# A projection's first column pair goes from eight block products to seven, and all four pairs start with the products on the first half of x

## The chip, the cores and the metric

The kernel runs on one core of a Trainium2 chip. Its metric is the time of one execution on the device, in microseconds (us). The profile is that of one execution; its times are counted from the first instruction. TensorE appears as PE, its weight loads as PEld, VectorE as DVE, ScalarE as ACT, GpSimd as POOL, SyncE's DMA queue as SPq.

## The reference

One decoder layer on 1024 prompt rows and 8 sample rows of 1024 channels. Everything starts from one normalised input and one combined projection, whose columns are cut into seven parts of 1024:

```python
xn = _rmsnorm(h, pre_g)
proj = jnp.einsum('bld,de->ble', xn, w_in)
u, v, z_a, x_b, z_b, g_a, g_b = jnp.split(proj, SPLITS, axis=-1)
u = jax.nn.gelu(u)
vn = _layernorm(jax.nn.gelu(v), ln_g, ln_b)
y_a = u * _chunk_spatial_mix(vn, w_s, b_s) * jax.nn.silu(z_a)
...
m = (jax.nn.sigmoid(g_a) * jnp.einsum('ble,ed->bld', y_a, w_pa)
     + jax.nn.sigmoid(g_b) * jnp.einsum('ble,ed->bld', y_b, w_pb))
h = h + _rmsnorm(jnp.einsum('bld,de->ble', m, w_out), post_g)
e = jnp.einsum('blp,pd->bld', p, w_ple)
gate = jax.nn.sigmoid(jnp.einsum('bld,de->ble', _rmsnorm(h, ple_in_g), w_pg))
h = h + _rmsnorm(gate * e, ple_out_g)
```

The change is in the projection to v, the first of the seven to be computed.

## The kernel before

**Products.** Each part of the projection is made in four *pairs* of 256 output channels. For a pair the weights are a 2x2 grid of blocks (A11 to A22: two halves of 128 output channels by two halves of 512 input channels) and x, held transposed in the tile `big`, a 2x2 grid too (B11, B21: prompt rows 0 to 511; B12, B22: rows 512 to 1023 and the 8 sample rows, 520 columns). One block product (`product`) is 12 matmuls of 512 columns, or 24 of 260 for the wide right half, because each operand is cut (`split`) into a high and a low part and three of the four combinations are summed. ACT writes the high part, DVE the low.

**Strassen and classical.** `strassen` makes a pair in seven products, P1 to P7, in place of eight. It needs sums of weight blocks (S1 to S4, DVE, in `Weights.prepare`) and sums of x blocks (T1 to T4: `Operand.combine` on DVE, then `Operand.cut`). The T sums are made once and serve every pair of all seven parts; they can only be made once all of x has been normalised and turned. So pair 0 of v goes through `classical` instead: eight products, two at a time into one PSUM tile, first the two on the first half of x (A11·B11 + A12·B21, then the same with A21 and A22), later the two on the second half. ACT copies each of the four sums to the output tile. Pairs 1 to 3 of v, and all later parts, go through `strassen`, where P1's result is copied by ACT to a tile `u`, DVE adds P6 and P7 to it, and three more DVE adds give the outputs.

**The opening, written out by hand.** `begin` fixes the order of each engine up to about 44 us: loads, the embedding product for rows 0 to 511 (`embed`, `embed_out`), the square sums, roots and scalings of the x rows (`norm_root`: square on ACT, a DVE addition, a power on POOL; `norm_scale` on DVE), their transposes (`x_half`: PE into PSUM, ACT writes the high part, DVE the low part), and the copies that rebuild the whole of x in `big` (`x_out` on ACT from PSUM, `x_whole` on POOL from the two parts). `x_extra` turns the 8 sample rows, `p_turn` the rows of p, `x_tail` cuts the 8 sample columns. Pair 0's first two sums run between the first and the second half of x.

**PSUM.** There are three regions (`region`, two banks each) and two single banks (`bank`). A new tile takes the one whose last user comes first in the program, and waits for that user (`Planner.wanted`):

```python
over = [(max(o.seq for o in self.users[n]), n) for n in live]
old = min(x for x in over if x[0] < first.seq)[1]
first.before.update(self.users[old])
```

**After the opening** a planner (`Planner.order`) orders each engine's instructions by due times; PE's may pass each other where their data allow. `run_stream` asks for weights six steps ahead (`FETCH`) and prepares operands three steps ahead (`AHEAD`). All SBUF tiles of this phase are drawn from 46 slots of one row each. Finished pairs of v are turned to token order by copies to 16-bit planes on ACT, transposing DMAs, and copies back to `big` (`v_planes`, `v_join`, `v_turn`).

Of the kernel before, what the change touches and what calls it, by code (L numbers as in the profile page):

```python
# [15 lines left out]
P = 128  # L16
# [291 lines left out]
def hybrid_step(  # L308
# [199 lines left out]
    class Weights:  # L508
# [13 lines left out]
        def sums(self):  # L522
            if not self.kept:
                self.kept = [slot(f"{self.name}s", (P, 2, 4, P)) for _ in range(2)]
            return self.kept

        def prepare(self, what):

            w = slot(f"{self.name}w", (P, 2, 4, P), F32R)
            hi, lo = w[:, 0], w[:, 1]  # L530
            if what[0] == "A":
                split(self.quarter(int(what[1]) - 1, int(what[2]) - 1), hi, lo)
            elif what == "S2":
                s1, s4 = self.sums()
                add(s1[:, 0], self.quarter(1, 0), self.quarter(1, 1))
                sub(s1[:, 1], s1[:, 0], self.quarter(0, 0))
                sub(s4[:, 0], self.quarter(0, 1), s1[:, 1])
                split(s1[:, 1], hi, lo)
            elif what == "S3":
                s3 = self.sums()[1][:, 1]  # L540
                sub(s3, self.quarter(0, 0), self.quarter(1, 0))
                split(s3, hi, lo)
            else:
                split(self.sums()[0 if what == "S1" else 1][:, 0], hi, lo)
            self.ready[what] = hi, lo

    class Features:
# [72 lines left out]

    def classical(weights, operand, user):

        steps, regions = [], {}
        for j in range(2):
            for m in range(2):
                names = [f"A{m + 1}{k + 1}" for k in range(2)]

                def prepare(names=names):
                    for n in names:
                        if n not in weights.ready:  # L630
                            weights.prepare(n)

                def run(names=names, j=j, m=m):
                    first = m == j == 0
                    ps = regions[m, j] = bank("acc").unsqueeze(1) if first else region("acc")
                    for i, n in enumerate(names):
                        product(Features, ps, weights.ready[n], operand, f"B{i + 1}{j + 1}", i == 0, i == 1,
                                late=m == 0)

                def evacuate(j=j, m=m):  # L640
                    user.direct(m, j, Features.view(regions[m, j], j == 1))

                steps.append(Step(prepare, run, evacuate))
        steps[0].loads = lambda: (weights.fetch(), user.loads())
        steps[-1].after.append(user.finish)
        return steps

    def strassen(weights, operand, user, form=Features, order=None):
# [6 lines left out]
                ("P3", "S4", "B22", "r4"))  # L655
        place = {p: r for p, _, _, r in plan}
        halved = order is not None and order[-1] == "P2"

        def evacuate(p):
            ps = None if halved and p == "P1" else form.view(at[place[p]], p not in ("P1", "P2", "P4"))  # L660
            if p == "P1":
                both = slot("u", form.sums)
                at["u"], at["u7"] = both[:, 0], both[:, 1]
                if form.tail:
                    nc.gpsimd.memset(at["u"][:, HALF:], 0.0)
                for i, c in enumerate(CUTS if halved else ()):
                    nc.scalar.activation(out=at["u"][:, c], in_=at["r1"][i][:, :QUART], func=AF.Copy)
                if not halved:
                    nc.scalar.activation(out=at["u"][:, :HALF], in_=ps, func=AF.Copy)
                return  # L670
            u, u7 = form.like(at["u"]), form.like(at["u7"])
            if p == "P6":
                add(u, ps, u)
                at["whole"] = True
                if "r3" in at:
                    evacuate("P7")
            elif p == "P2":
                user.direct(0, 0, ps)
            elif p == "P7":
                if "whole" in at:  # L680
                    add(u7, ps, u)
            elif p == "P5":
                user.summed(1, 1, ps, u7, u7)
            elif p == "P4":
                user.summed(1, 0, ps, at["u7"][:, :HALF])
            else:
                user.summed(0, 1, ps, u)

        for p, a, b, r in sorted(plan, key=lambda x: order.index(x[0])) if order else plan:
            def run(p=p, a=a, b=b, r=r):  # L690
                new = r not in at
                if new:
                    at[r] = form.new()
                product(form, at[r], weights.ready[a], operand, b, new, True, not new)

# [10 lines left out]
            steps.append(Step(lambda a=a: weights.prepare(a), run_halves if halved and r == "r1" else run, done))  # L706
        steps[0].loads = lambda: (weights.fetch(), user.loads())
        steps[-1].after.append(user.finish)
        return steps

    class User:
# [7 lines left out]
        def loads(self):  # L719
            pass  # L720

        def outs(self):
# [134 lines left out]
    def x_half(j, kp):  # L857

        if kp == (NB // 2 - 1 if j else 0):
            ps = [bank("pst") for _ in range(2)]  # L860
        else:
            ps = region("pst")
            ps = [ps[:, kk] for kk in range(2)]
        for kk in range(2):
            k = 2 * kp + kk
            for i in range(4):
                nc.tensor.transpose(ps[kk][:, i * P : (i + 1) * P], xts[4 * j + i][:, k * P : (k + 1) * P], ident)
        hi, lo = x_parts(j, kp)
        for kk in range(2):
# [31 lines left out]
    def x_tail():  # L901
        for kp in range(NB // 2):
            split(quarter(kp, 1)[:, :, HALF:], *(x[:, :, HALF:] for x in x_parts(1, kp)))
# [42 lines left out]
    class V(User):  # L946
        turns = [[7, 0, 1], [2, 3, 4], [5, 6]]

    lnv = {}
# [328 lines left out]
    vsteps, vusers, vweights = [], [], []  # L1278
    for i, (w, u) in enumerate(pairs_of(V0, V, "v")):
        vsteps.append((strassen if i else classical)(w, xop, u))  # L1280
        vusers.append(u)
        vweights.append(w)
# [25 lines left out]
    every = lambda groups: [s for g in groups for p in g for s in p]  # L1308
    steps = [s for p in vsteps + gasteps for s in p] + every(usteps)
    late = []  # L1310
# [6 lines left out]

    c = vsteps[0]
    at(c[0], lambda: xop.combine("T3"))
    at(c[0], lambda: (xop.combine("T1"), xop.combine("T2")))  # L1320
    at(c[1], lambda: xop.cut("T2"))
    at(c[1], lambda: xop.combine("T4"))
    at(c[2], lambda: xop.cut("T3"))
    at(c[3], lambda: xop.cut("T1"))
    at(vsteps[1][0], lambda: xop.cut("T4"))

# [3 lines left out]
    for i, u in enumerate(vusers):  # L1330

        nxt = vsteps[1][1:] + vsteps[2] if i == 0 else (vsteps[i + 1] if i + 1 < NPAIR else gasteps[0])
        at(nxt[0], lambda u=u, i=i: v_turn(u.out, i, [S]))
        at(nxt[0], lambda u=u, i=i: v_planes(u.out, i))
        for m in range(2):
            at(nxt[2 + m], lambda u=u, i=i, m=m: v_join(u.out, i, m))
        for s, ts in zip(nxt[4:], V.turns):
            at(s, lambda i=i, ts=ts: v_turn(None, i, ts))
# [383 lines left out]
    def begin():  # L1722
# [9 lines left out]
        dma(xe[:NS], x_sample)  # L1732
        steps[0].loads()
        for t in range(4, NB):
            x_load(t)
# [3 lines left out]
        praw.append(psl)  # L1739
        steps[4].loads()  # L1740
        fetched[0] = 5
        early_loads()
# [5 lines left out]

        for h in range(2):
            p_new(h)  # L1750
        busy(5)
# [39 lines left out]
        for kp in range(3):  # L1791
            x_half(0, kp)
        vweights[0].prepare("A12")
        x_half(0, 3)
        steps[0].run()
        steps[1].prepare()
        norm_root(4)
        norm_root(S)
        norm_root(5)
        norm_scale(4)  # L1800
        norm_root(6)
# [5 lines left out]
        x_whole(0, 1)  # L1807
        steps[0].evacuate()
        x_out(0, 3)
        x_out(0, 2)  # L1810
        steps[1].run()
        x_extra()
        steps[1].evacuate()
        p_turn(1, 0)
        x_half(1, 0)
        p_turn(1, 1)
        x_half(1, 1)
        x_tail()
        embed(4)
        x_half(1, 2)  # L1820
        x_whole(1, 0)
        embed_out(4)
        x_half(1, 3)
        x_whole(1, 1)
        x_out(1, 2)
        x_out(1, 3)
        embed(5)
        embed_out(5)
        prepared[0] = 4
        steps[2].run()  # L1830
        steps[2].evacuate()
        embed(6)
        embed_out(6)

# [10 lines left out]
    plan.fixed = False  # L1845
    for s in range(3):
        for f in steps[s].after:
            f()
    at(steps[3], embed_rest)
    at(steps[8], embed_rows)  # L1850
    at(steps[14], embed_sample)
    run_stream(steps, 3)
    plan.play(tc)
# [30 lines left out]
```

## Time and profile before

| | |
|---|---|
| median of 3 runs | 977.66 us (977.46 to 977.98) |
| the profiled execution | 978.18 us |
| its span, first to last instruction | 976.1 us |
| PE busy in the span | 965.9 us |
| mean granted TensorE clock | 0.998 of full speed |

An engine is busy while an instruction of it runs. The span leaves out 2.08 us of the execution's own time. A row of the timeline gives the start, the duration, the engine, the operation and its tiles, and in brackets the idle time of the engine before it with what ended it; a row with "xN" merges N neighbours of one kind, and its duration runs from the first's start to the last's end.

### The profile page before, as it was taken

Reading aid. Unit: us, or ns where it says so; the run is one execution under the profiler, and the core shown is the slowest. Engines: PE = TensorE matmul, PEld = TensorE weight load, DVE = VectorE, ACT = ScalarE, POOL = GpSimd, SP = SyncE. Lnnn points to the kernel's source line nnn. Section 1 sums busy time; section 2 is a strip of 40 time slices with the busy share of each in tenths; the row PEclk is TensorE's granted clock in tenths of the full one; section 3 lists DMA queues with packets and bytes.
Section 4 is the critical chain, followed back from the end, with each engine's and each line's share of the span. In section 5 each row is a group of like instructions: output and inputs, shape, how many; then the busy total and the mean of one; then the engine's idle time right before and its main releaser. Section 6 shows DMA issues by size and latency. Waiting matters only on the chain. (4 is left out here: it accounts for less than half of the span.)

```text
span 976.1 us, 16062 instructions
## 1 busy us (share of the span) xinstructions
PE 965.9 (99%) x6089; PEld 861.1 (88%) x6089; DVE 797.1 (82%) x1256; ACT 530.7 (54%) x897; POOL 78.7 (8%) x144
## 2 busy tenths in 40 slices
PE   9999999999999999999999999999999999999996
PEld 6898999999999999999999999999999986888775
DVE  6894768777789698979797987697699899769786
ACT  6888997565434333344443343552363273977662
POOL 1500000000000000001000100000000000312222
PEclk9999999999999999999999999999999999999999
DMA  9437354322483353766735076884583392899876
GB/s 330 144 120 181 91 153 152 111 99 78 141 287 130 105 188 108 249 196 216 257 132 181 30 248 231 278 309 152 177 302 105 131 348 88 176 282 363 262 216 194
DMA packets 111914, 183.97 MB, mean 188 GB/s; under 512 B 28959, under 2 KB 68343, under 8 KB 111830
## 3 DMA queue, kind: packets, MB, share of 16 engines
q1 hardware_dynamic: 109710, 175.53, 53.0%
q0 software_dynamic: 2080, 7.41, 4.2%
q8 instruction: 48, 0.79, 0.3%
q14 instruction: 28, 0.23, 0.1%
q10 hardware_dynamic: 48, 0.01, 0.0%
HBM read 124.27 MB, written 53.87 MB: 182 GB/s over the span
## 5 line engine op out<-in xcount | busy, mean ns | idle before, releaser
L301 DVE TENSOR_TENSOR u<-acc,u 128x520 f32<-128x520 f32 (+1 forms) x90 | 62.4, 694 | 31.9 <-PE acc L301 29.3
L301 POOL TENSOR_TENSOR rstd<-ms,mhalf 128x1 f32<-128x1 f32 (+1 forms) x36 | 30.3, 843 | 225.4 <-DVE ms L301 225.1
L301 POOL MEMSET u<- 128x8 f32 x35 | 3.7, 108 | 502.9 <-PE acc L301 235.3
L301 ACT ACTIVATE u<-acc 128x512 f32<-128x512 f32 x39 | 23.3, 597 | 25.9 <-PE acc L301 25.1
L301 ACT ACTIVATE paw<-pas 128x512 fp32r<-128x512 f32 x16 | 10.1, 628 | 30.9 <-DVE pas L301 25.6
L301 ACT ACTIVATE pbw<-pbs 128x512 fp32r<-128x512 f32 x16 | 9.9, 628 | 28.6 <-DVE pbs L301 25.4
L301 DVE TENSOR_TENSOR big<-big 128x1024 f32<-128x1024 f32 (+4 forms) x20 | 23.6, 1211 | 0.0
L301 ACT ACTIVATE big<-mix 128x256 f32<-128x256 f32 x32 | 12.0, 383 | 18.6 <-PE mix L301 18.0
L301 PE MATMUL accm<-qh,wpoolw 128*128 128x260 f32 (+1 forms) x96 | 21.0, 320 | 0.0
L301 ACT ACTIVATE big<-v 128x1024 uint16<-128x1024 uint16 x16 | 18.3, 1174 | 3.0 <-DMA v<-vw 3.0
L301 ACT ACT_TABLE_LOAD x13 | 16.7, 1283 | 5.1 <-PE acc L301 2.7
L301 ACT ACTIVATE zbw<-zbs 128x512 fp32r<-128x512 f32 x16 | 10.1, 628 | 16.8 <-DVE zbs L301 10.5
L301 DVE TENSOR_TENSOR acc<-acc,u 128x512 f32<-128x512 f32 (+1 forms) x16 | 11.1, 696 | 8.8 <-PE acc L301 8.8
L301 ACT ACTIVATE gbw<-gbs 128x512 fp32r<-128x512 f32 x16 | 10.0, 626 | 14.7 <-DVE gbs L301 12.5
L301 DVE TENSOR_TENSOR big<-mix,big 128x256 f32<-128x256 f32 x32 | 12.8, 420 | 6.1 <-ACT big L301 5.6
L301 PEld LDWEIGHTS accm<-qh,wpoolw 128*128 128x128 f32 x96 | 15.6, 188 | 1.9
L301 ACT ACTIVATE zaw<-zas 128x512 fp32r<-128x512 f32 x16 | 10.1, 628 | 13.2 <-PE acc L301 5.2
L301 ACT ACTIVATE gb<-gb 128x1032 f32<-128x1032 f32 (+1 forms) x8 | 6.8, 853 | 19.1 <-DVE gb L301 19.1
L301 ACT ACTIVATE u<-u 128x1032 f32<-128x1032 f32 (+1 forms) x8 | 6.8, 853 | 18.9 <-DVE u L301 18.8
L301 ACT ACTIVATE uw<-us 128x512 fp32r<-128x512 f32 x16 | 10.0, 627 | 12.6 <-DVE us L301 8.3
L301 ACT ACTIVATE za<-za 128x1032 f32<-128x1032 f32 (+1 forms) x8 | 6.8, 855 | 17.4 <-DVE za L301 17.3
L301 ACT ACTIVATE vw<-v 128x1024 uint16<-128x1024 uint16 x16 | 16.0, 1045 | 0.0
(674 smaller groups left out, 3607.6 us busy)
## 6 DMA issues: line engine op xcount, KB each, us to landing
ga<-ga SPq DMA_DIRECT2D x16, 516.0 KB
gb<-gb SPq DMA_DIRECT2D x16, 516.0 KB
ya<-za SPq DMA_DIRECT2D x8, 516.0 KB
yb<-zb SPq DMA_DIRECT2D x8, 516.0 KB
x<-in_x_prompt_dram SPq DMA_DIRECT2D x8, 512.0 KB
vraw<-in_w_in_dram SPq DMA_DIRECT2D x8, 512.0 KB
e<-e SPq DMA_DIRECT2D x8, 512.0 KB
garaw<-in_w_in_dram SPq DMA_DIRECT2D x8, 512.0 KB
```

The costliest lines, as they stand in the source:

```text
L301: getattr(getattr(self.nc, e), method)(*args, **kwargs)
```

## The change

Pair 0 of v is made by `strassen` too, and `classical` goes. All four pairs take a new order, `AHEAD_OF` = P1, P2, P6, P7, P4, P5, P3. P1 and P2 need only B11 and B21, the first half of x: they run for pairs 0 and 1 in the opening, where pair 0's first two sums stood, and for pairs 2 and 3 right behind the opening, before any product on a T sum. P1 and P2 share a single bank; between them ACT copies P1 into the second half of the pair's own output tile (`V.sum_in`), where it waits for P6, and after P2 ACT copies the finished block to the first half. The weights come as two sides of 128 output channels (`Sides`); pairs 1 to 3 load the first side twice. B12 is no longer cut, since no product uses it: the second half of x's first four channel blocks is only copied to `big`, by ACT from PSUM, and the two `x_whole` on POOL for it go. Pair 0's weight sums and T3 are made at the end of the opening.

```diff
+        def add_up(self):
+            self.added = True
+            s1, s4 = self.sums()
+            add(s1[:, 0], self.quarter(1, 0), self.quarter(1, 1))
+            sub(s1[:, 1], s1[:, 0], self.quarter(0, 0))
+            sub(s4[:, 0], self.quarter(0, 1), s1[:, 1])
...
+    class Sides(Weights):
...
+        def side(self, m):
+            self.sides[m] = slot(f"{self.name}raw", (P, 2, 4, P))
+            for k in range(2):
+                dma(self.sides[m][:, k], self.src[k * HALF : (k + 1) * HALF, m * P : (m + 1) * P]
+                    .rearrange("(k p) m -> p k m", p=P))
+
+        def fetch(self):
+            for m in range(0 if self.again else 1, 2):
+                self.side(m)
...
+    AHEAD_OF = ("P1", "P2", "P6", "P7", "P4", "P5", "P3")
...
-                    at[r] = form.new()
-                product(form, at[r], weights.ready[a], operand, b, new, True, not new)
+                    at[r] = bank("acc").unsqueeze(1) if ahead and r == "r1" else form.new()
+                product(form, at[r], weights.ready[a], operand, b, new, True, not new, late=ahead and p == "P1")
...
-        if kp == (NB // 2 - 1 if j else 0):
+        if kp == 0:
             ps = [bank("pst") for _ in range(2)]
...
+        if j and kp < 2:
+            turned[j, kp] = ps
+            return
...
-        for kp in range(NB // 2):
+        for kp in range(2, NB // 2):
             split(quarter(kp, 1)[:, :, HALF:], *(x[:, :, HALF:] for x in x_parts(1, kp)))
...
     class V(User):
         turns = [[7, 0, 1], [2, 3, 4], [5, 6]]
+
+        def sum_in(self, i, form):
+            self.out = [*(self.out or ()), slot(self.key)]
+            return self.out[i][:, HALF:]
...
-    steps = [s for p in vsteps + gasteps for s in p] + every(usteps)
+    steps = [vsteps[i][j] for pairs in ((0, 1), (2, 3)) for j in range(2) for i in pairs]
+    steps += [s for p in vsteps for s in p[2:]] + [s for p in gasteps for s in p] + every(usteps)
...
-        vweights[0].prepare("A12")
+        vweights[1].prepare("A11")
         x_half(0, 3)
         steps[0].run()
-        steps[1].prepare()
+        vweights[0].prepare("A12")
+        vweights[1].prepare("A12")
         norm_root(4)
+        steps[0].evacuate()
+        steps[1].run()
         norm_root(S)
         norm_root(5)
+        steps[1].evacuate()
         norm_scale(4)
...
-        steps[0].evacuate()
+        steps[2].run()
+        steps[2].evacuate()
         x_out(0, 3)
         x_out(0, 2)
-        steps[1].run()
+        steps[3].run()
+        for t in (8, 4, 5):
+            steps[t].loads()
+        steps[8].loads = None
         x_extra()
-        steps[1].evacuate()
+        steps[3].evacuate()
+        p_new(1)
         p_turn(1, 0)
-        x_half(1, 0)
+        x_half(1, 2)
         p_turn(1, 1)
-        x_half(1, 1)
+        x_half(1, 3)
         x_tail()
         embed(4)
-        x_half(1, 2)
-        x_whole(1, 0)
-        embed_out(4)
-        x_half(1, 3)
-        x_whole(1, 1)
         x_out(1, 2)
+        x_half(1, 0)
+        x_out(1, 0)
+        embed_out(4, nc.vector)
         x_out(1, 3)
+        x_half(1, 1)
+        x_out(1, 1)
+        vweights[0].add_up()
+        xop.combine("T3")
         embed(5)
         embed_out(5)
         prepared[0] = 4
-        steps[2].run()
-        steps[2].evacuate()
-        embed(6)
-        embed_out(6)
```

## Rows read from the trace of the kernel before

**Rows 1.** The page's first part: each engine's busy time, share and instructions.

```profile
PE 965.9 (99%) x6089; PEld 861.1 (88%) x6089; DVE 797.1 (82%) x1256; ACT 530.7 (54%) x897; POOL 78.7 (8%) x144
```

**Rows 2.** Windows: stretch, length, busy PE, PEld, DVE, ACT, POOL; clock, DMA share, GB/s.

```profile
44.00:62.00 18.00, 18.00 (x126) 16.79 (x125) 18.00 (x23) 13.00 (x21) 0.01 (x1) 1.00 0.30 112
62.00:100.00 38.00, 38.00 (x252) 33.66 (x251) 25.67 (x36) 33.42 (x60) 1.10 (x1) 1.00 0.61 153
100.00:150.00 50.00, 50.00 (x343) 45.91 (x342) 35.38 (x62) 46.43 (x95) 1.67 (x4) 1.00 0.45 118
```

**Rows 3.** Timeline of PE: first matmuls of P5, P1, P3 and P6 in v.

```profile
75.49 0.40 PE L301 MATMUL acc<-xT1h,vw 128*128 128x260 f32 x2
...
78.37 0.39 PE L301 MATMUL acc<-xB11h,vw 128*128 128x512 f32 x1
...
81.15 0.40 PE L301 MATMUL acc<-xB22h,vw 128*128 128x260 f32 x2
...
84.03 0.40 PE L301 MATMUL acc<-xT2h,vw 128*128 128x260 f32 x2
```

**Rows 4.** Timeline of PE in and behind the opening (p_turn twice, embed twice, P6).

```profile
33.86 0.66 PE L301 MATMUL pp<-ident,p 128*128 128x128 f32 x4
...
35.58 0.60 PE L301 MATMUL pp<-ident,p 128*128 128x128 f32 x4
...
36.81 0.48 PE L301 MATMUL e<-wehi,ph 128*128 128x512 f32 x1
...
41.32 0.48 PE L301 MATMUL e<-wehi,ph 128*128 128x512 f32 x1
...
63.98 0.40 PE L301 MATMUL acc<-xT2h,vw 128*128 128x260 f32 x2
```

**Rows 5.** Timeline of ACT in the opening.

```profile
25.30 1.09 ACT L301 ACTIVATE squares<-x 128x1024 f32<-128x1024 f32 x1
...
30.50 0.57 ACT L301 ACTIVATE v<-acc 128x512 f32<-128x512 f32 x1
30.98 2.37 ACT L301 ACTIVATE big<-pst,gvec 128x512 f32<-128x512 f32 x4
33.44 0.60 ACT L301 ACTIVATE v<-acc 128x512 f32<-128x512 f32 x1
...
37.41 1.28 ACT L301 ACTIVATE xB12h<-pst,gvec 128x512 fp32r<-128x512 f32 x2
```

**Rows 6.** Timeline of DVE in the opening.

```profile
14.93 1.22 DVE L301 COPY e<-e 128x1024 f32<-128x1024 f32 x1
...
30.71 4.21 DVE L301 TENSOR_SCALAR x<-x,rstd 128x1024 f32<-128x1024 f32 x3
34.84 0.40 DVE L301 TENSOR_TENSOR big<-pxe,gvec 128x16 f32<-128x16 f32 x4
...
39.01 1.40 DVE L301 SCALAR_TENSOR_TENSOR xB12l<-pst,gvec,xB12h 128x512 fp32r<-128x512 f32 x2
```

**Rows 7.** The tile x: its scalings on DVE, ns min/median/max.

```profile
L301 DVE TENSOR_SCALAR x<-x,rstd x8: 744/752/2725, 13.9 to 32.2; 128x1024 f32<-128x1024 f32 x8
```

**Rows 8.** Timeline of POOL in the opening: two of the four x_whole.

```profile
31.84 5.32 POOL L301 TENSOR_TENSOR big<-xB11h,xB11l 128x1024 f32<-128x1024 f32 x2
```

**Rows 9.** Timeline of DVE behind the opening.

```profile
46.68 6.92 DVE L301 TENSOR_TENSOR big<-big 128x1040 f32<-128x1040 f32 x6
...
61.26 2.38 DVE L301 TENSOR_TENSOR xT3l<-big,xT3h 128x1040 fp32r<-128x1040 f32 x2
...
69.40 1.22 DVE L301 TENSOR_TENSOR xT1l<-big,xT1h 128x1040 fp32r<-128x1040 f32 x1
...
78.58 0.70 DVE L301 TENSOR_TENSOR v<-acc,u 128x520 f32<-128x520 f32 x1 [0.99 <-PE acc L301]
```

**Rows 10.** Groups of DVE, 62 to 150 us: count, busy us, mean ns, idle before.

```profile
L301 DVE TENSOR_TENSOR vw<-vs,vw 128x512 fp32r<-128x512 f32 x11 | 7.3, 679 | 0.7 <-ACT vw L301 0.7
```

More of the change, by code (lines that the diff above doesn't have):

```diff
@@ L525, in sums @@
             return self.kept
+        added = False
+        def add_up(self):
[4 more added lines that the diff above has]
+            sub(s4[:, 0], self.quarter(0, 1), s1[:, 1])
         def prepare(self, what):
@@ L533, in prepare @@
             elif what == "S2":
[L534 to L538, printed above, removed]
+                if not self.added:
+                    self.add_up()
+                split(self.kept[0][:, 1], hi, lo)
             elif what == "S3":
@@ L545, in prepare, with __init__, quarter @@
             self.ready[what] = hi, lo
+    class Sides(Weights):
+        def __init__(self, src, name, again=True):
+            super().__init__(src, name)
+            self.again, self.sides = again, {}
+        def side(self, m):
[6 more added lines that the diff above has]
+                self.side(m)
+        def quarter(self, m, k):
+            return self.sides[m][:, k]
     class Features:
@@ L619, in hybrid_step @@
     nothing = lambda: None
[L621 to L646, printed above, removed]
+    AHEAD_OF = ("P1", "P2", "P6", "P7", "P4", "P5", "P3")
     def strassen(weights, operand, user, form=Features, order=None):
@@ L656, in strassen @@
         place = {p: r for p, _, _, r in plan}
+        ahead = order == AHEAD_OF
         halved = order is not None and order[-1] == "P2"
@@ L661, in evacuate @@
             if p == "P1":
-                both = slot("u", form.sums)
-                at["u"], at["u7"] = both[:, 0], both[:, 1]
+                at["u"] = user.sum_in(0, form)
+                if not ahead:
+                    at["u7"] = user.sum_in(1, form)
                 if form.tail:
@@ L670, in evacuate @@
                 return
-            u, u7 = form.like(at["u"]), form.like(at["u7"])
+            if p == "P7" and ahead:
+                at["u7"] = user.sum_in(1, form)
+            u = form.like(at["u"])
+            u7 = form.like(at["u7"]) if "u7" in at else None
             if p == "P6":
@@ L706, in strassen @@
             steps.append(Step(lambda a=a: weights.prepare(a), run_halves if halved and r == "r1" else run, done))
-        steps[0].loads = lambda: (weights.fetch(), user.loads())
+        if ahead:
+            steps[0].loads = lambda: weights.side(0)
+            steps[2].loads = lambda: (weights.fetch(), user.loads())
+        else:
+            steps[0].loads = lambda: (weights.fetch(), user.loads())
         steps[-1].after.append(user.finish)
@@ L720, in loads @@
             pass
+        def sum_in(self, i, form):
+            if i == 0:
+                self.both = slot("u", form.sums)
+            return self.both[:, i]
         def outs(self):
@@ L947, in hybrid_step, with sum_in @@
         turns = [[7, 0, 1], [2, 3, 4], [5, 6]]
+        def sum_in(self, i, form):
+            self.out = [*(self.out or ()), slot(self.key)]
+            return self.out[i][:, HALF:]
     lnv = {}
@@ L1278, in hybrid_step @@
     vsteps, vusers, vweights = [], [], []
-    for i, (w, u) in enumerate(pairs_of(V0, V, "v")):
-        vsteps.append((strassen if i else classical)(w, xop, u))
+    for i in range(NPAIR):
+        w, u = Sides(inp(V0, i), "v", i > 0), V(i, "v")
+        vsteps.append(strassen(w, xop, u, order=AHEAD_OF))
         vusers.append(u)
@@ L1315, in hybrid_step @@
     steps += [s for p in gbsteps[1:] + pasteps + pbsteps for s in p]
[L1318 to L1325, printed above, removed]
+    at(steps[3], lambda: (xop.combine("T1"), xop.combine("T2")))
+    at(steps[4], lambda: xop.cut("T2"))
+    at(steps[5], lambda: xop.cut("T3"))
+    at(steps[6], lambda: (xop.combine("T4"), xop.cut("T4")))
+    at(steps[7], lambda: xop.cut("T1"))
     at(vsteps[2][3], ln_loads)
@@ L1330, in hybrid_step @@
     for i, u in enumerate(vusers):
-        nxt = vsteps[1][1:] + vsteps[2] if i == 0 else (vsteps[i + 1] if i + 1 < NPAIR else gasteps[0])
+        nxt = [s for p in vsteps[i + 1 :] for s in p[2:]] + gasteps[0]
         at(nxt[0], lambda u=u, i=i: v_turn(u.out, i, [S]))
@@ L1733, in begin @@
         steps[0].loads()
+        steps[1].loads()
         for t in range(4, NB):
@@ L1739, in begin @@
         praw.append(psl)
-        steps[4].loads()
-        fetched[0] = 5
+        fetched[0] = 6
         early_loads()
@@ L1747, in busy @@
                 nc.tensor.matmul(ps, junk[:, :P], junk, start=True, stop=True)
-        for h in range(2):
-            p_new(h)
+        p_new(0)
         busy(5)
@@ L1845, in hybrid_step @@
     plan.fixed = False
-    for s in range(3):
+    for s in range(4):
         for f in steps[s].after:
             f()
[L1849 to L1852, printed above, removed]
+    embed(6)
+    embed_out(6)
+    at(steps[4], embed_rest)
+    at(steps[9], embed_rows)
+    at(steps[15], embed_sample)
+    run_stream(steps, 4)
     plan.play(tc)
```

## The prediction

> **What bounds the kernel now.** I read the page's first part first: PE is busy 965.9 of 976.1 us, and no other engine comes near [rows 1]. The windows then ask whether that holds in each stage. It does: from 44 to 150 us PE is busy in every microsecond, at full clock; DVE is busy all of 44 to 62 as well, and ACT 46.43 of the 50 us after 100 [rows 2]. So a matmul taken out shortens the run by its own time, a wait put in lengthens it by its own, and there is no idle time of PE to win. The waits that could come are in two places: the hand-ordered opening, where PE, ACT and DVE feed each other with almost no play, and the stretch behind it, where DVE makes the T sums. For these I read the three timelines side by side, from one instruction to its successor on the next engine.
>
> My sum is made against the profiled execution, 978.18 us (its span of 976.1 and 2.08 outside it). The median of the runs, 977.66, lies 0.52 lower, and that goes off at the end. A measurement of this kernel can tell about 0.2% from no change, which is 1.96 us.
>
> **What is removed.** Eight products become seven, three on 512 columns and four wide ones in place of four and four: one narrow product goes. In a stream without waits the next product's first matmul follows a narrow one after 81.15 - 78.37 = 2.78 us, a wide one after 2.88 [rows 3]. That is -2.78 us, and it is all that PE saves: transposes and embedding products are the same in number, and the products put ahead are only moved.
>
> Cutting B12 goes too: four DVE instructions of about 0.7 [rows 6] and four on ACT, with their tails. ACT gets four copies of about 0.6 for the two `x_whole` dropped from POOL [rows 5], so its load is about the same. None of this is on PE; what it is worth I count where DVE is short.
>
> **The opening: what is added, and who waits.** PE's work there is the same as before up to `x_extra`: four narrow products. But four results leave PSUM in place of two. P1 of each of the two pairs must be copied by ACT before P2 may add to its bank, and these two copies stand in ACT's queue between the square sums of x rows 4 to 7. ACT runs there without a gap, from the square at 25.30 to the copy at 33.44 [rows 5]. A copy takes 0.48 (30.50 to the next start at 30.98), so the square of row 7, and all behind it, comes 1.0 us later.
>
> Row 7's scaling is the last of the three in the DVE row that ends at 34.92 [rows 6]. It is the slow one of the eight, 2.73 us against a median of 0.75 [rows 7], and beside it runs POOL's `x_whole`, from 31.84 [rows 8]; I take it that DVE is held up by POOL. Both come 1.0 later, so the scaling ends at 35.9 and the sample rows' gains (0.40, right behind it) at 36.3.
>
> Now the PSUM banks. `p_turn(1, 0)` needs one, and both have users: P2 of pair 1, copied out by ACT at 33.44 + 1.0 + 0.6 = 35.0, and `x_extra`, read by those gains until 36.3. By the planner's rule the tile whose last user stands first in the program gives way, and `x_extra`'s gains stand ahead of pair 1's copy. So `p_turn(1, 0)` waits for DVE and starts at 36.4, against 33.86 before [rows 4]. If it were the other bank, it would start at 35.2, but then the transposes behind it wait for row 7 until 36.0. The waiting instruction holds all of PE: its order is fixed.
>
> From there I follow two chains to `embed(5)`. A `p_turn` and a half, twelve transposes, took 36.81 - 35.58 = 1.23 [rows 4], so `x_half(1, 2)` ends at X = 36.4 + 1.23 = 37.6; before, the first such half ended at X = 35.58. PE's own work from X to `embed(5)` is the same as before in sum, 41.32 - 35.58 = 5.74. The other chain: two high parts, p's and two more on ACT end at X + 3.1 (37.41 + 1.28 = 38.69 before [rows 5]), the low parts on DVE at X + 4.8 (39.01 + 1.40 = 40.41 [rows 6]), two small tails at about X + 5.1, and then comes `embed_out(4)`, now on DVE, 1.22 by the one at 14.93. `embed(5)` takes that copy's region, the first to come free, so it starts at X + 6.45 with 0.15 for the signal: 44.05 in place of 41.32. The opening gives back 2.7 us. With the other bank X is 36.55 and it gives back 1.7. I take 2.4, nearer to the first, which follows from the rule in the code.
>
> **Behind the opening.** Before T2 is needed PE has three embedding products and four narrow ones, each twelve matmuls of 512 columns: 7 x 2.78 = 19.5 us, so with 2.4 given back P6 comes at 43.7 + 19.5 = 63.2 (63.98 before [rows 4]); then every 2.88 or 2.78 us P7 (T3), P4 (T4) and P5 (T1, at 71.8). DVE needs for these from the start of T3's sums at about 45.7: sixteen instructions of about 1.15 for the four sums and four low parts, 18.5 with T2's tails; eleven of 0.6 (0.68 long, each started 0.6 after the last) for the first weights of pairs 2 and 3, S2, S3, A22, S1 and two additions, 6.6 [rows 9, 10]. That ends at 70.8, 1.0 ahead of P5; before, T1 was done at 70.6 for a P5 at 75.49 [rows 3, 9]. Play shrinks from 5 us to 1, but no wait follows. Pair 0's other work on DVE (sums, more splits, five adds in place of ACT's copies, about 8 us) falls in 62 to 100, where DVE idles 12 of 38 us [rows 2].
>
> The weight loads are the same megabyte in the same place of SPq's queue, and pairs 2 and 3 load early; the second load of the first sides is spread over 45 us with the DMA engines at 0.61 and 0.45 [rows 2]. I cost them at nothing; ACT's square of row 4 at 25.30 covers the x rows queued behind them, and if those came late it would shift the same chain one for one. The conversion of v starts some 10 us later, and ACT is nearly full. But the P1 and P2 copies and high parts of pairs 2 and 3 have gone ahead of it, and nothing on PE waits for v before the mixing.
>
> I add 0.2 for small waits behind the opening. Sum: 978.18 - 2.78 + 2.4 + 0.2 = 978.0, less 0.52 is 977.5; with the two ends of the opening 976.8 and 977.8. I forecast 977.4, between them, no difference that can be told.
>
> **Rivals.** *The opening gives back little.* If row 7's scaling gets through ahead of POOL, it takes 0.75, not 2.73, and ends near 34.0. Then `p_turn(1, 0)` starts at 34.5, X is 35.7, and `embed(5)` follows at X + 6.45 = 42.15, or at X + 5.74 = 41.45 if `embed_out(4)` is not late: 0.1 to 0.8 given back, 978.18 - 2.78 - 0.52 + these = 975.0 to 975.7. For it: POOL's power for row 7 and `x_whole` are no longer driven back to back, because ACT's copies now stand between the squares. Against it: both DVE and POOL wait for the same square as before. The Trainium skill states the rule (SBUF — State Buffer, "Who interferes with whom"): a DVE operation in a two-port mode, which a scaling can take, and a GpSimd operation exclude each other, and whoever issues first holds the ports to its end. By that rule the outcome hangs on which starts first; the 2.73 beside 0.75 agrees with POOL having been first here.
>
> *PE waits at the end of each pair: slower.* P3 adds to P5's region and must wait for DVE's add on it. Before, the next pair's P1 stood between them: P5 at 75.49, P1 at 78.37, P3 at 81.15 [rows 3]. P1 is now gone ahead; only the next pair's P6 can stand there, and it needs three weight sums and a split from DVE, two steps earlier than before, from weights that are asked for six steps ahead and must find slots. Where P6 is late, P3 waits for DVE's add: by the one at 78.58, which ran 0.70 behind PE's end near 78.5 [rows 9], with the signals 1.0 us. Pair 0's place is the tightest: DVE is done with T1 at 70.8 and has some 3.5 us left to do for a P6 due at 74.7, so it decides from where DVE is half a microsecond behind these times and stays so. There are three such places (behind pair 3 the next part's P1 stands), so the price is 3 us: 979.8 to 980.9 from the forecast's two ends. Against it: from the second pair on DVE has some 9.5 us to do in the 14 of five products.
>
> *The change doesn't do what it says.* It does: seven products follow from the code.
>
> **Chances.** Forecast 0.50, little given back 0.28, slower 0.22. The first rival lies below 975.7, the limit for faster; the second lies over the limit of 979.6. The forecast's own range, 976.3 to 978.4, is inside both. About one in ten left out at each end, somewhere inside either rival, gives 975.2 to 979.9. Faster 0.29, same 0.49, slower 0.22.
>
> **What would show it.** PE's matmuls fall by 12 in the 512-column form. `p_turn(1, 0)` and `embed(5)` start 1.7 to 2.7 later than at 33.86 and 41.32; ACT's square of row 7 ends 1.0 later; row 7's scaling still takes over 2 us. PE has gaps only there. If P6 of pair 0 starts near 63 and P5 follows 8.6 later, DVE kept up. I am wrong if x row 7 is ready before 35, if `p_turn(1, 0)` waits for neither bank, or if PE shows gaps of about 1 us before the P3s.

## The result and the profile after

The changed kernel takes 980.18 us at the median of 17 runs (978.27 to 981.84); the kernel before, beside it on the same chips, 977.89 (977.36 to 978.65). The ratio is 1.0021, with a 95% interval of 1.0013 to 1.0028: slower by 2.3 us, where 977.4 and a range up to 979.9 had been forecast. Four of the 17 runs show a mean granted clock of 0.998 and take 978.3 to 979.0 us, the other thirteen show 0.995 or 0.996 and take 979.0 to 981.8; the profiled run is one of the latter, with 980.18 us, a span of 978.4 (978.38 in the trace, 976.14 before) and a clock of 0.996.

The first part of the page of the changed kernel, which answers to [rows 1]:

```profile
PE 964.9 (99%) x6077; PEld 860.4 (88%) x6077; DVE 799.1 (82%) x1263; ACT 532.3 (54%) x899; POOL 73.2 (7%) x143
```

Twelve matmuls fewer, as forecast, and PE is busy 1.0 us less in a span 2.3 longer. So PE stands still, or works slowly, somewhere. The timeline of PE in the changed kernel, beside [rows 4]:

```profile
33.32 0.66 PE L301 MATMUL pxe<-ident,xe 8*128 8x8 f32 x8
36.30 1.09 PE L301 MATMUL pp<-ident,p 128*128 128x128 f32 x4 [2.32 <-issue]
37.17 1.91 PE L301 MATMUL pst<-ident,x 128*128 128x128 f32 x8
38.88 0.85 PE L301 MATMUL pp<-ident,p 128*128 128x128 f32 x4
...
45.11 0.50 PE L301 MATMUL e<-wehi,ph 128*128 128x512 f32 x1
...
64.70 0.40 PE L301 MATMUL acc<-xT2h,vw 128*128 128x260 f32 x2
...
73.26 0.41 PE L301 MATMUL acc<-xT1h,vw 128*128 128x260 f32 x2
```

Read it against [rows 4] line by line. `p_turn(1, 0)` starts at 36.30 in place of 33.86, behind 2.32 us of idle time: that is the forecast wait, forecast for 36.4. Then something else: the same p_turn and half transpositions take 38.88 - 36.30 = 2.58 us, where the second p_turn and half took 1.23 before. `embed(5)` starts at 45.11: 3.79 later, not 2.7. The windows of this stretch (length, busy PE, PEld, DVE, ACT, POOL; clock; DMA share; GB/s) show where that time goes:

```profile
33.00:36.00 3.00, 0.98 (x10) 0.57 (x8) 2.93 (x5) 1.81 (x4) 3.00 (x3) 0.99 0.86 228
36.00:38.00 2.00, 1.71 (x8) 1.74 (x9) 0.19 (x3) 0.52 (x1) 2.00 (x1) 0.50 0.08 15
38.00:40.00 2.00, 2.00 (x15) 2.00 (x13) 0.69 (x1) 0.95 (x3) 0.66 (x18) 0.66 0.01 4
40.00:42.00 2.00, 2.00 (x13) 1.74 (x12) 1.57 (x3) 2.00 (x5) 0.00 (x0) 1.00 0.00 0
```

The third number from the end is the granted clock of TensorE. From 36 to 38 us it is 0.50, the 1.2 GHz level, and in part of the next two microseconds as well; before and behind it is 1.00, the 2.4 GHz level. It falls as the idle stretch ends, and PE pays for the wait a second time. That the idle time is what lets it fall is not shown by these rows; two experiments below test it.

Why PE waited stands on ACT, DVE and POOL. ACT in the changed kernel, beside [rows 5]:

```profile
28.92 0.57 ACT L301 ACTIVATE v<-acc 128x512 f32<-128x512 f32 x1
29.40 1.04 ACT L301 ACTIVATE squares<-x 128x1024 f32<-128x1024 f32 x1
...
30.44 1.05 ACT L301 ACTIVATE squares<-x 128x1024 f32<-128x1024 f32 x1
```

DVE, beside [rows 6]:

```profile
31.69 4.18 DVE L301 TENSOR_SCALAR x<-x,rstd 128x1024 f32<-128x1024 f32 x3
35.79 0.41 DVE L301 TENSOR_TENSOR big<-pxe,gvec 128x16 f32<-128x16 f32 x4
```

POOL, beside [rows 8]:

```profile
32.82 5.26 POOL L301 TENSOR_TENSOR big<-xB11h,xB11l 128x1024 f32<-128x1024 f32 x2
```

All as forecast to a tenth: the copy of P1 (`v<-acc`) stands between the squares, the three scalings end at 35.87 (forecast 35.9), the sample rows' gains at 36.20 (36.3), and PE's transposition of p starts behind them.

**The ledger.** Two more points of PE's timeline are needed: T4 of the last pair of v, and PE's last matmul. In the changed kernel:

```profile
115.48 0.48 PE L301 MATMUL acc<-xT4h,vw 128*128 128x512 f32 x1
...
969.37 0.28 PE L301 MATMUL last<-wgB21h,hw 128*128 128x256 f32 x1
```

In the kernel before:

```profile
114.42 0.40 PE L301 MATMUL acc<-xT4h,vw 128*128 128x512 f32 x1
...
967.63 0.28 PE L301 MATMUL last<-wgB21h,hw 128*128 128x256 f32 x1
```

Up to `embed(5)` the changed kernel loses 3.79. From there to T4 of the last pair it takes 115.48 - 45.11 = 70.37 in place of 114.42 - 41.32 = 73.10: -2.73, the narrow product. From there to PE's last matmul it takes 853.89 in place of 853.21: +0.68. From that matmul to the end of the last DVE instruction (at 974.64 after, at 972.92 before) it takes 5.27 in place of 5.29: -0.02. From there to the span's end it takes 3.74 in place of 3.22: +0.52. The sum is +2.24, the difference of the spans, 978.38 - 976.14.

The last DVE instruction ends the chain of waits. The last row of that chain in the changed kernel (DVEq is DVE's sequencer):

```profile
973.98 0.66 DVEq L1909
```

Of the +0.68 only 0.2 had been forecast, and of the +0.52 nothing. So four things were to be tested: the bank's wait, the slow scaling, the clock, and what lies behind the opening.

### The profile page after: what moved, and what is told of

Read it like the earlier page. It is cut to its first block, busy times and chain, and to the rows that moved or that the text cites. A ratio compares the mean times of both kernels' runs of the same rounds, so it can differ in the third digit from the quotient of the medians.

```text
span 978.4 us, 16078 instructions
## 1 busy us (share of the span) xinstructions
PE 964.9 (99%) x6077; PEld 860.4 (88%) x6077; DVE 799.1 (82%) x1263; ACT 532.3 (54%) x899; POOL 73.2 (7%) x143
## 5 line engine op out<-in xcount | busy, mean ns | idle before, releaser
L301 DVE TENSOR_TENSOR u<-acc,u 128x520 f32<-128x520 f32 (+1 forms) x84 | 58.3, 695 | 23.8 <-PE acc L301 21.9
L301 DVE TENSOR_TENSOR v<-acc,v 128x520 f32<-128x520 f32 (+1 forms) x20 | 13.9, 693 | 12.8 <-PE acc L301 12.6
```

The source lines that it names most:

```text
L301: getattr(getattr(self.nc, e), method)(*args, **kwargs)
```

## The experiments

All are made from the changed kernel, but two (`e7_gap`, `e11_old_tail`) from the one before. The opening as a whole starts at other times in other executions: `x_extra`'s first transposition stands at 33.27 before, at 33.32 after, and between 32.63 and 33.73 in the experiments. So openings are compared by the time from there to `embed(5)`: 8.05 before, 11.79 after.

**PE kept busy in the gap.** Nine matmuls on unused data, whose result nobody reads, stand in the gap:

```diff
         x_extra()
+        busy(9)
```

> Nine dummy matmuls, whose results nobody reads, stand behind x_extra in PE's order, so PE works in the 2.3 us before p_turn(1, 0). Theory (the wait for the gains costs about 2.4 us, and the idle PE then runs at half its clock, which costs another 1.35): the granted clock stays near 1.00 from 36 to 40 us, p_turn(1, 0) still starts near 36.3 to 36.5, it and the half behind it take about 1.25 us in place of 2.58, embed(5) starts near 43.8 to 44.0 in place of 45.1, and the run takes 1.2 to 1.35 us less than after. Rival (the clock falls for another reason than the idle PE, as the transposes' shape): the clock shows 0.50 again, embed(5) stays at 45.1 or later, no gain. Second rival (the lost time comes from behind the opening): embed(5) comes earlier but the run's time stays.

Measured: 978.80 us (11 runs, 978.19 to 979.63), ratio to before 1.0009 (95% interval in brackets, here and below: [1.0000, 1.0017]); 1.38 less than after. PE:

```profile
33.63 2.12 PE L301 MATMUL warm<-junk 128*128 128x512 bf16 x9
35.95 0.63 PE L301 MATMUL pp<-ident,p 128*128 128x128 f32 x4 [0.20 <-PE warm L301]
...
37.28 0.60 PE L301 MATMUL pp<-ident,p 128*128 128x128 f32 x4
...
43.47 0.51 PE L301 MATMUL e<-wehi,ph 128*128 128x512 f32 x1 [0.17 <-DVE e L301]
```

The windows of that run:

```profile
36.00:38.00 2.00, 2.00 (x19) 2.00 (x20) 0.69 (x1) 1.11 (x2) 2.00 (x11) 1.00 0.36 86
38.00:40.00 2.00, 2.00 (x14) 1.75 (x13) 1.22 (x2) 2.00 (x5) 0.31 (x10) 1.00 0.01 2
```

The wait is as long as it was (`x_extra` to `p_turn(1, 0)` 2.91 in place of 2.98), and yet the p_turn and half behind it take 1.33 in place of 2.58, at a clock of 1.00; `embed(5)` comes 10.43 behind `x_extra` in place of 11.79, -1.36. The idle PE is what let the clock fall. All 11 runs of this kernel show a mean clock of 0.997 or 0.998. The four runs of the changed kernel with 0.998, 978.3 to 979.0 us, lie where this kernel lies; that the clock stayed up in these four is inferred from this, since only one run of the changed kernel was profiled.

**The same gap in the old kernel.** One more transposition ahead of `p_turn(1, 0)`, of a tile that POOL's second `x_whole` writes:

```diff
         steps[1].evacuate()
+        nc.tensor.transpose(region("late")[:, 0, :P], quarter(1, 0)[:, 0, :P], ident)
         p_turn(1, 0)
```

> The kernel before, unchanged but for one more transposition ahead of p_turn(1, 0), of the tile that POOL's second x_whole writes (until 37.2), whose result nobody reads: PE idles there from about 34 to 37.2 in the old kernel. Theory (an idle PE alone, without any of the change, drops the granted clock): the clock shows 0.50 for some microseconds behind the gap, the p_turn and half behind it take about 2.5 in place of 1.23, embed(5) comes 4.5 to 4.8 later than at 41.32 and the run is about 4.7 longer than the kernel before, 982 to 982.7. Rival (the idle time costs only itself): embed(5) 3.4 later, 981.2, clock 1.00 throughout. It also gives a second profile of the old kernel's later stages: if PE's stretch from pair 3 of v to the end of the products takes 0.6 less than in the changed kernels here too, that difference belongs to the program; if it takes as long as theirs, the one profile of before was short there by chance.

Measured: 982.60 us (5 runs, 982.26 to 983.29), ratio 1.0044 [1.0032, 1.0057], 4.5 more than the runs of before beside it. PE and, below, the windows:

```profile
36.56 0.48 PE L301 MATMUL late<-ident,big 128*128 128x128 f32 x1 [3.23 <-POOL big L301]
36.83 1.06 PE L301 MATMUL pp<-ident,p 128*128 128x128 f32 x4
...
39.39 0.67 PE L301 MATMUL pp<-ident,p 128*128 128x128 f32 x4
...
45.21 0.48 PE L301 MATMUL e<-wehi,ph 128*128 128x512 f32 x1
```

```profile
36.00:38.00 2.00, 1.44 (x7) 1.44 (x8) 0.00 (x0) 0.01 (x1) 0.51 (x1) 0.53 0.00 0
38.00:40.00 2.00, 2.00 (x13) 2.00 (x12) 0.69 (x1) 0.95 (x2) 0.00 (x0) 0.62 0.02 4
```

A `p_turn` and a half take 2.56 us here, with the same fall of the clock to half and with nothing of the change in the kernel; `embed(5)` comes 12.54 behind `x_extra`, +4.5 for an idle time of 3.2. This kernel settles a second point: from T4 of the last pair to PE's last matmul it takes 853.21, as the kernel before does. So the 853.21 of before was not chance, and the 0.68 that the changed kernel loses there goes with its program.

**The bank.** `p_turn(1, 0)` takes a PSUM region that is free, in place of the bank that `x_extra`'s gains hold:

```diff
-        ps = bank("pp").rearrange("p (k c) -> p k c", k=2)
+        ps = (region("pp")[:, 0] if (h, q) == (1, 0) else bank("pp")).rearrange("p (k c) -> p k c", k=2)
```

> p_turn(1, 0) takes a PSUM region in place of the bank that x_extra's gains hold until 36.2. Theory (that bank is what it waits for): p_turn(1, 0) starts near 34 to 35, x_half(1, 2) then waits for x's row 7, whose scaling still ends at 35.9, X (the end of that half) is near 36.5 in place of 38.88, and the gap of PE is split in two, so that the clock stays up or falls for less; embed(5) near 42.9 and about 2 us less than after, 978 or a little under. Rival (x row 7 alone decides, the bank is no matter): x_half(1, 2) starts no earlier than before, the clock falls all the same, embed(5) at 44.5 or later and under 0.6 us gained.

Measured: 977.52 us (977.05 to 978.12), ratio 0.9998 [0.9989, 1.0006]. PE:

```profile
33.37 0.66 PE L301 MATMUL pp<-ident,p 128*128 128x128 f32 x4
33.86 0.49 PE L301 MATMUL pst<-ident,x 128*128 128x128 f32 x3
35.30 0.77 PE L301 MATMUL pst<-ident,x 128*128 128x128 f32 x5 [0.94 <-DVE x L301]
```

Now `p_turn(1, 0)` waits for nothing, and the half behind it waits 0.94 for the scaled row 7, which the profile names as what ended the wait. So the wait of the changed kernel was the bank's. `embed(5)` is 9.30 behind `x_extra`, -2.5, of which 1.4 is the shorter wait; the rest goes with the clock, which stays at 1.00:

```profile
36.00:38.00 2.00, 2.00 (x17) 1.87 (x16) 0.77 (x2) 1.90 (x4) 2.00 (x18) 1.00 0.26 64
```

**POOL behind the scaling.** POOL copies one column of the scaled row 7, which nobody reads, and so its two `x_whole` start behind that scaling:

```diff
             norm_scale(t)
+        nc.gpsimd.tensor_copy(out=sm("behind"), in_=xts[7][:, :1])
         x_whole(0, 0)
```

> POOL gets one copy of a column of the scaled row 7 ahead of its two x_whole additions, so these start behind that scaling. Theory (POOL's additions hold the scaling up): row 7's scaling takes 0.75 in place of about 2.7 and ends near 34.0, the gains near 34.3, p_turn(1, 0) starts near 34.4 in place of 36.3, PE's gap is under half a microsecond and the clock stays up, embed(5) near 42.1, and the run is about 3 us shorter than after, near 977.2. Rival (the scaling is slow for its own reasons, or waits for ACT's square chain): the scaling still takes over 2 us and p_turn(1, 0) stays at 36 or later. Second rival (x_whole is now late): x_extra or the products behind wait for POOL's additions and the gain is lost there.

Measured: 977.10 us (976.21 to 978.08), ratio 0.9993 [0.9984, 1.0001]. The tile x, its scalings on DVE (ns minimum, median, maximum), against [rows 7]:

```profile
L301 DVE TENSOR_SCALAR x<-x,rstd x8: 744/753/754, 13.9 to 33.1; 128x1024 f32<-128x1024 f32 x8
```

POOL and PE in the same run:

```profile
34.04 0.19 POOL L301 COPY behind<-x 128x1 f32<-128x1 f32 x1 [0.93 <-DVE x L301]
34.18 4.71 POOL L301 TENSOR_TENSOR big<-xB11h,xB11l 128x1024 f32<-128x1024 f32 x2
```

```profile
34.50 0.63 PE L301 MATMUL pp<-ident,p 128*128 128x128 f32 x4 [0.56 <-PE pxe L301]
...
42.02 0.51 PE L301 MATMUL e<-wehi,ph 128*128 128x512 f32 x1 [0.17 <-DVE e L301]
```

The slowest scaling takes 0.754 in place of 2.7, so POOL's addition did hold it up, and POOL's own two take 4.71 in place of 5.26. `embed(5)` is 8.73 behind `x_extra`. This is the case that the first rival of the forecast described, reached by an edit. The Trainium skill (SBUF — State Buffer, "Who interferes with whom") says that a DVE operation in a two-port mode and a GpSimd operation exclude each other and the first to issue holds the ports; that agrees with 2.7 beside 0.754 here.

**ACT relieved.** DVE makes the two copies of P1, and ACT's squares stand one behind the other. The copies also move ahead in the written order, in front of the square sums that they stood behind:

```diff
-                if not halved:
+                if ahead and user.pair < 2:
+                    nc.vector.tensor_copy(out=at["u"][:, :HALF], in_=ps)
+                elif not halved:
                     nc.scalar.activation(out=at["u"][:, :HALF], in_=ps, func=AF.Copy)
...
         steps[0].run()
+        steps[0].evacuate()
         vweights[0].prepare("A12")
         vweights[1].prepare("A12")
         norm_root(4)
-        steps[0].evacuate()
         steps[1].run()
         norm_root(S)
+        steps[1].evacuate()
         norm_root(5)
-        steps[1].evacuate()
```

> The two copies of P1 are made by DVE in place of ACT, ahead of the norms, so the squares of rows 4 to 7 on ACT run without them. Theory (ACT's two copies shift the whole chain by 1.0, and the slow scaling and the bank behind it stay): the square of row 7 is 1.0 earlier, row 7's scaling ends near 34.9 and still takes over 2 us, p_turn(1, 0) starts near 35.3, the gap of PE is 1.3 us, the clock may fall for a shorter time or not at all; embed(5) at 42.9 to 44.1 and 1 to 2.2 us less than after. Rival (DVE is as short as ACT there): the norms wait behind the copies and p_turn(1, 0) stays near 36.3.

Measured: 978.40 us (977.10 to 980.13), ratio 1.0005 [0.9996, 1.0014]. PE:

```profile
35.77 0.63 PE L301 MATMUL pp<-ident,p 128*128 128x128 f32 x4 [1.38 <-issue]
```

`x_extra` to `embed(5)` is 9.56, -2.2, with `x_extra` itself 0.4 later at 33.73. Row 7's scaling still takes 2.72. The profile shows the clock at 1.00 behind a gap of 1.38:

```profile
36.00:38.00 2.00, 2.00 (x21) 2.00 (x20) 0.69 (x1) 1.29 (x3) 2.00 (x16) 1.00 0.21 53
```

But the runs spread over 3 us, and four of the eleven, the four slowest, show a mean clock of 0.995 or 0.996. So this profile does not say that the clock stays up behind such a gap in every execution.

**Both mends of the opening** (region and POOL):

> Both single mends together: p_turn(1, 0) takes a region in place of the bank, and POOL's x_whole additions come behind row 7's scaling. Theory (the opening's loss is the sum of the bank's wait and of the scaling slowed by POOL): p_turn(1, 0) starts near 33.4, x_half(1, 2) waits for row 7 until about 34.1 only, X is near 35.2, embed(5) at 41.4 to 41.6, and the run is about 0.5 shorter than with POOL's part alone, near 976.6. Rival (either mend alone took all there was, embed_out(4) on DVE now sets embed(5)): embed(5) stays at 42.0 and the run at 977.1.

Measured: 976.19 us (975.52 to 977.64), ratio 0.9979 [0.9970, 0.9988]. PE:

```profile
33.46 0.66 PE L301 MATMUL pp<-ident,p 128*128 128x128 f32 x4
...
34.82 0.60 PE L301 MATMUL pp<-ident,p 128*128 128x128 f32 x4
...
41.00 0.50 PE L301 MATMUL e<-wehi,ph 128*128 128x512 f32 x1 [0.16 <-DVE e L301]
```

No wait is left ahead of `embed(5)` but 0.16 for `embed_out(4)`; 8.13 behind `x_extra`, 0.08 more than before. **With the copies on DVE as well:**

> As the run before, and the two copies of P1 are made by DVE, so ACT's squares stand one microsecond earlier. Theory (each of the three parts adds to the opening's loss): row 7's scaling ends near 33.0 to 33.4, PE has no gap before X, X is near 34.8, embed(5) near 41.0 to 41.3 as in the kernel before or earlier, and the run lies near 976.2. Rival (the chain of copies behind X, high parts on ACT, low parts and embed_out(4) on DVE, sets embed(5)): embed(5) stays at 41.4 to 42.0, no gain over the run before this one. Second rival (DVE's copies delay the norms' scalings): X later than 35.2.

Measured: 976.37 us (975.94 to 977.88), ratio 0.9984 [0.9975, 0.9993]; `embed(5)` at 41.22, again 8.13 behind `x_extra`. The first rival held in what matters, no gain: once the two other mends are in, ACT's copies cost nothing, and the third mend gains nothing. (41.22 lies in the theory's range, but so does the 41.00 of the run before, without this mend.)

**The end.** The ledger's last term, the time behind the last DVE instruction, lies in what SP does at the end. In every trace its transfers, but for the first few, take eight semaphores in turn, and at the end SP waits for these eight in one fixed order and then comes to its drain instruction. From the traces (us; "its place" is that of the last transfer in this order, and the last column is the time from the end of its wait to the drain):

```
kernel        SP transfers  last one issued  its place  its wait over  drain   behind it
before        385           972.95           4th        975.00         975.37  0.37
after         399           974.67           2nd        976.75         977.60  0.85
e8_tail       405           971.23           8th        973.27         973.40  0.13
e9_mended     405           970.45           8th        972.50         972.63  0.13
e11_old_tail  389           972.41           8th        974.46         974.59  0.13
```

The last three rows are experiments described below. Issue to landing is the same 2.04 to 2.08 everywhere; what stands behind it in the order is paid for. The change adds 14 transfers, so the last one moved two places forward and 0.48 more stands behind it. Only 0.13 of that is the two places, at some 0.06 each. The rest is one step of SP, right behind the last transfer's wait, that takes 0.39 in place of 0.06, although in the changed kernel the semaphores that it names had been raised long before, at 959.69 and 924.01. It takes 0.39 in all seven profiles with this order, and why is open. Six tiny loads near 100 us, added to the kernel with POOL's part mended, move it to the last place:

```diff
     def ln_loads():
+        extra = cpool.tile([1, 6 * NB], F32, tag="extra", name="extra")
+        for i in range(6):
+            dma(extra[:, i * NB : (i + 1) * NB], ln_g[:1, :NB])
```

> The kernel with POOL's part mended, and six more tiny loads on SP's queue near 100 us, which nobody reads, so that SP issues 405 transfers in place of 399 (385 in the kernel before). Theory (SP's transfers take eight semaphores in turn, at the end SP waits for them in a fixed order, and what stands behind the last landing is paid: the 14 added transfers moved the last one from the fourth place to the second, 0.37 to 0.85 us behind it): the last two transfers now have the last two places, the time from the last DVE instruction's end to the span's end falls from 3.0 by 0.5 to 0.8, and the run is 0.5 to 0.7 shorter than with POOL's part alone, near 976.5. Rival (the end's length is chance): no difference, 977.1.

Measured: 976.14 us (975.38 to 978.70), ratio 0.9981 [0.9972, 0.9990], against 0.9993 [0.9984, 1.0001] for the kernel without the loads: 1.2 us by the ratios, with intervals that overlap. The trace shows 0.72 of it at the end (from the last DVE instruction's end to the span's end 2.97 in place of 3.73, which is the stretch that the expectation gives as 3.0); `x_extra` to `embed(5)` is the same 8.72, but the opening began 0.66 earlier in this execution, so the rest need not be the loads'.

**The old kernel with its end moved** (the same edit with four loads):

> The kernel before with four tiny loads that nobody reads near 100 us, so that its last two transfers take the last two of the eight semaphores as well. Theory: from the last transfer's wait to the drain 0.13 in place of 0.37, and 0.2 to 0.3 less than the kernel before, about 977.7; so the end was worth 0.25 to the old kernel and 0.7 to the changed one. Rival (the extra loads cost more on SP's queue than the end gives): 977.9 or more.

Measured: 977.61 us (977.12 to 978.62), ratio 0.9998 [0.9990, 1.0007]. In the trace 0.13 in place of 0.37, as expected; in the runs 0.3 less, which is within what they scatter.

**All mends that helped** (region, POOL, six loads):

> The region for p_turn(1, 0), POOL's additions behind row 7's scaling, and six tiny loads that nobody reads. Theory (the opening and the end are separate losses, so the mends add): PE as in the run with the two opening mends, embed(5) near 41.0; behind the last landing 0.13 in place of 0.85; 0.6 to 0.7 less than with the two opening mends, near 975.5, and 2.3 to 2.5 less than the kernel before, the 2.78 of the product less what cannot be told from here. Rival (the end's gain was the chip's jitter): 976.2, no difference.

Measured: 975.43 us (974.99 to 976.70), ratio 0.9975 [0.9966, 0.9984], 2.5 less than before, where the change as it was made is 2.3 more. `embed(5)` is 8.13 behind `x_extra`. This version beats both kernels. What the six loads add to the two mends of the opening is 0.72 in the trace (0.13 behind the wait in place of 0.85), but 0.4 by the ratios, with intervals that overlap: the end's gain is shown by the traces, and the runs alone do not tell it from nothing.

## Why the prediction was wrong

**Right: what is removed.** -2.78 was forecast from the spacing of products, -2.73 measured between `embed(5)` and T4 of the last pair, with no wait between them. P6 at 64.70 and P5 at 73.26 are 8.56 apart (forecast 8.6). DVE had T1's low parts done at 70.36, 2.9 us ahead of P5, where the forecast left 1.0: from `embed(5)` DVE took 25.3, not the 27.1 that the forecast's times give, since only eight of the eleven weight instructions counted stood there. So play shrank less than forecast. The slower rival, P3 waiting at three pair ends, did not come. (Its price of 3 us on the forecast's two ends gives 979.8 to 980.8, not 980.9. The measured 980.18 lies in that stretch, but not for that rival's reason: the trace has no wait of PE there.)

**Right: which waits the opening gets, and why.** The copies on ACT, the scaling beside POOL, the gains, the bank that follows from the rule in the code: each time within 0.1 us of the forecast; and without the bank's wait, without POOL beside the scaling, or without the copies on ACT, PE went on earlier each time. The rival in which little is given back did not come by itself, since POOL was first again; POOL's mend made its case, and the run took 977.1, not the 975.0 to 975.7 forecast for it, because the losses named below come on top: 0.81 between T4 of the last pair and PE's last matmul, 0.52 at the end, and the 0.52 of the median.

**Wrong: the step "The opening gives back 2.7 us ... I take 2.4".** It measured 3.79. The failing link is X: "A `p_turn` and a half, twelve transposes, took 36.81 - 35.58 = 1.23 [rows 4], so `x_half(1, 2)` ends at X = 36.4 + 1.23 = 37.6". They took 2.58, because the wait that the paragraph before it puts ahead of them leaves PE idle for 2.32 us and the granted clock falls to half. The premise stands in the prediction's first paragraph, "a wait put in lengthens it by its own": filling the same gap gave back 1.36, and a gap of 3.2 in the old kernel cost 4.5. X came at 38.88; from there `embed(5)` followed after 6.23 (forecast 6.45). The text took a duration measured on a busy PE and put it behind an idle one. Choosing 2.4 under the computed 2.7 made it worse by 0.3: the bank followed from the code, and there was nothing to hedge.

**Wrong in size: "I add 0.2 for small waits behind the opening".** 0.68 was lost there, and the profile shows no idle time of PE in that stretch. About half of it lies in matmuls that both kernels have in the same order: from 201 us of the kernel before to PE's last matmul, nine profiles of the new order take 766.95 to 767.04 between the same two matmuls and three of the old order 766.62 to 766.66. The rest lies between 115 and 201 us, where the two orders differ. Over the whole stretch from T4 of the last pair the nine take 853.63 to 854.44 (two of them with one wait of PE, of 0.29 and 0.11) and the three 853.21 to 853.23. That the loss goes with the program is shown; its size changes with each program, and its cause stays open.

**Missed: the end.** The end took 0.52 more behind the last DVE instruction, of which 0.48 is what stands behind the last transfer in SP's order. And the 0.52 between the profiled execution and the median of before did not come off again: the profiled run of the changed kernel is its median.

Together: 1.39 in the opening, 0.05 that the product gave less than forecast, 0.48 behind the opening, 0.52 at the end and 0.52 for the median, less 0.02 ahead of the last DVE instruction's end and 0.24 because 1.80 us lie outside this span and 2.04 outside that of before, are 2.70: the distance from the forecast's sum, 977.48, to the result, 980.18.

## What to carry to other kernels

A wait put on the engine that sets the end is not to be priced by its own length alone: ask at which clock that engine runs when it comes back, and price the instructions behind the wait at that level (here 2.3 us of waiting cost 3.7: the wait, and the 1.36 that came back when the gap was filled). When a hand-ordered stretch is rearranged, follow for each new wait which buffer it is on, because another buffer, or the order of two engines that hold each other up, can take the whole wait away: two edits of one line each turned a loss of 2.3 us into a gain of 1.9. And a change that alters the number of transfers can move the end of the kernel by half a microsecond without touching it, as the traces here show.

## What was not expected of the hardware

- PE at half its clock behind an idle stretch of 2.32 us in a kernel that is at 1.00 for 30 us before it and for 930 us behind it (windows of the changed kernel), and probably not in every execution: four of 17 runs show a mean clock of 0.998.
- The time from a single matmul to the next repeats to a few nanoseconds in profiles of one order and changes with the order: one of `xB11h,zbw` near 441 us lasts 0.225 to 0.226 us until the next in all three profiles of the old order, and 0.240 to 0.241 in all nine of the new. Why is open.
- What stands behind the last transfer in the order in which SP waits at the end costs 0.13 to 0.85 us. In the order of the changed kernel one step behind the last landing took 0.39 in place of the 0.06 of its neighbours, in all seven profiles with that order; why is open.
